# LayerNorm statistics of a dense decoder part: per-token transposes replaced by GpSimd sums and products with 1/1024

## The chip, the cores and the metric

The kernel runs on one core of a Trainium2 chip. The metric is the device time of one execution in microseconds (us), the median of the runs of the same program. The profile is one execution seen by the hardware profiler; its engines are TensorE (PE; PEld is its weight load), VectorE (DVE), ScalarE (ACT), GpSimd (POOL) and SyncE (SP), which issues the DMAs.

## The reference, cut to what matters

Two decoder layers on x of 1024 tokens by 1024 channels, all in float32: layer 0 mixes tokens by a gated DeltaNet, layer 1 by a causal convolution of 31 taps; each is followed by an MLP.

```
def layer_norm(x, g, b):
    mu = mean(x, axis=-1); var = mean(square(x - mu), axis=-1)
    return (x - mu) * rsqrt(var + LN_EPS) * g + b

h = x * (1 + sc1) + sh1
y = deltanet_mixer(h, ...) if layer 0 else conformer_conv_mixer(h, ...)   # the second has a layer_norm of its own
x = layer_norm(ALPHA * x + (1 + gt1) * y, ln_g[i, 0], ln_b[i, 0])
h = x * (1 + sc2) + sh2
x = layer_norm(ALPHA * x + (1 + gt2) * (square(relu(h @ w1)) @ w2), ln_g[i, 1], ln_b[i, 1])
```

There are five LayerNorms in it. The last is done with the output; the four others are done here for each half of the tokens apart, which makes the eight that the change touches.

## The kernel before, in words

Activations lie transposed: a tile is 128 channels by 512 tokens, so eight tiles (k = 0 to 7) hold one half of the tokens (hf = 0 or 1). Each float32 product is done in three passes, with a weight tile split into `whi` and `wlo` and an activation split the same way (lines 234 to 236). A job is one weight tile of 128 by 1024: its load (`raw`), the cast `whi` on ACT, the rest `wlo` on DVE (line 415), 24 products of 512 columns on PE, and what empties the PSUM bank. One job is one unit of planned time (a tick). After the DeltaNet part the program is one list of such jobs: output projections (`dno0`, `dno1`), MLP up and down jobs, convolution inputs (`cfin`), convolution outputs (`cfo0`, `cfo1`). The taps of the convolution are 30 DVE instructions for each tile (line 961).

Every step of a job or a LayerNorm is an event with a planned time; the program sorts the events, and PE, DVE and ACT get their instructions in that order. Nothing waits for a planned time on the chip: each engine takes its instructions in order and waits only for data and buffers. POOL and SP also work in order; the order in which instructions stand there is made by the framework's scheduler.

The eight LayerNorms, in order of time, with the start of their transposes in the trace: `ln00_0` (650 us), `ln00_1` (702), `ln01_0` (1101), `lncf0` (1457), `ln01_1` (1502), `ln10_0` (1549), `lncf1` (1898), `ln10_1` (1993). The digits are layer, place in the layer and half; `cf` is the LayerNorm inside the convolution module. Each goes through these steps in `ln_job`:

- `tok(tt)`, four times: PE turns 128 tokens of the eight tiles round (eight transposes, line 982, four in one PSUM bank), DVE takes `bn_stats` of both banks and `bn_aggr` (lines 986 to 990), POOL makes rsqrt(var + eps) and -mean * rsqrt (lines 991, 256, 993) in columns of `lnst`.
- `rows_`: PE turns `lnst` into rows (line 1018), ACT copies them (1021), and three DMAs bring the rows through DRAM and back, spread over all partitions, as two tiles `lo` of 128 by 512.
- `back(k)`, eight times: DVE multiplies the tile by the first of these (1031) and adds the second (1033); `evac` makes the next activation on ACT (`hh`, the residual `ax`, and once more in `tl`; lines 1067 to 1073) and its rest on DVE (line 246).

While this goes on, PE works on the jobs of the other half. The table `LN` has for each LayerNorm the planned times of these steps, in ticks from its start t0. `resid` (line 259) adds a job's result to the residual tile `ax`. The mod jobs `ada` (line 202, DVE) stand among the first dense jobs.

Of the kernel before, what the change touches and what calls it, by code (L numbers as in the profile page):

```python
# [16 lines left out]
P = 128  # L17
D = 1024
# [71 lines left out]
}  # L90
TOK_AT = (0.0336, 0.0339, 0.0617, 0.4138)
ROWS_AT = (-0.2768, -0.2717)
BACK_AT = (-0.1782, 0.0453, 0.5048, 0.7384, 0.8678, 0.9365)
# [30 lines left out]
def tile_hybrid(ctx, tc, xT, c, adaT, cols, rows, gates, w_gate, w_first, w_dn, w_dno, w_cf, w_cfo,  # L124
# [24 lines left out]
    hb = Bufs("act", tz=3, lo=20)  # L149
    wb = Bufs("weights", raw=3, whi=2, wlo=2)  # L150
    cb = Bufs("const")
    sm = Bufs("small", st=2, mv=2, lnst=2, lnrow=2, rs=2, nb=2, ssk=2, ssq=2, nk=2, br2=6, eq=6, gl=6, ss=3)
    sm("pad", 96)
    dr = ctx.enter_context(tc.tile_pool(name="dr", bufs=1, space=DRAM))

# [723 lines left out]

    def res_post(ps, k, hf, l, j, v):  # L880
# [7 lines left out]
            yield  # L888
        return post

    def out_job(lab, w_dram, k, hf, l, t0, v):
        dense(lab, w_dram[k], t0, 1.0, wide_mm(hf, v), 4, (res_post(0, k, hf, l, 2, v), 1.0, RES_AT))

    def up_job(l, ci, f, hf, hid, t0):
# [32 lines left out]

    def dn_job(l, ci, q, hf, hid, t0):
        ends = (0.75 if q == 0 else 0.5, 1.0)
        dense(f"m{l}_dn{hf}", w_2[l, ci, q], t0, 1.0, hid_mm(hid, q == 0), 4,  # L930
              *[(res_post(j, q * 2 + j, hf, l, 5, ver(hf)), ends[j], RES_AT) for j in range(2)])

    def cf_job(hf, ct, t0):
# [9 lines left out]
        def post():  # L943
# [22 lines left out]
                yield  # L966
        at = max(t0 + 2 + CF_AT[2], conv_end[0])
        conv_end[0] = at + TAP[hf] * (CFK - 1)
        add(f"conv{hf}", post(), t0 + 2 + CF_AT[0], t0 + 2 + CF_AT[1], at,
            *spaced(at + 0.1, conv_end[0] + 0.1, CFK - 1))  # L970

# [91 lines left out]
    def ln_mod(lab, hf, l, which, t0):  # L1063
# [232 lines left out]
```

## Time and profile before

| | us |
|---|---|
| median of 3 runs | 2411.41 (2410.13 to 2414.36) |
| the profiled execution, whole | 2410.48 |
| its span, first to last instruction | 2408.6 |
| PE busy | 2357.5 (98%) |
| DVE busy | 1722.9 (72%) |
| ACT busy | 1100.3 (46%) |
| POOL busy | 409.3 (17%) |

Busy time is the union of an engine's instructions. Products on PE overlap: one of 512 columns shows about 390 ns, and yet 178 of them start in 40 us. So what one costs is read from start to start and not from its length. DVE instructions overlap a little as well (an instruction of 690 ns starts about 600 ns after the one before it). Idle time of an engine means loss only where PE, which has the most to do, stands still for it.

### The profile page before, as it was taken

To read this page: it belongs to the slowest core of one execution; us is meant where nothing else is said; L and a number is where in the kernel's file an instruction comes from. 1 tells how busy PE (TensorE), PEld (TensorE's weight loads), DVE (VectorE), ACT (ScalarE), POOL (GpSimd) and SP (SyncE) were. 2 spreads that over 40 slices of the span, in tenths; PEclk is the share of its full clock that TensorE was granted. 3 is DMA by queue.
4 is the path that set the end of the run, shared out by engine and by line. 5 is a ranking of instruction groups with operands and counts; after the bars stand their busy time and mean duration, and the time that the engine had idled before them with its cause. 6 is when DMAs were issued, how large, how long until landed. Compare 5 with 4: busy or idle time off the path is not lost.

```text
span 2408.6 us, 33443 instructions
## 1 busy us (share of the span) xinstructions
PE 2357.5 (98%) x12730; PEld 1946.2 (81%) x12730; DVE 1722.9 (72%) x2712; ACT 1100.3 (46%) x1949; POOL 409.3 (17%) x841
## 2 busy tenths in 40 slices
PE   8899999999999999999999999999999999999998
PEld 6677878787778888888888888878888888888887
DVE  6667677676686566656899998799888766444447
ACT  4767767564256333335433334563333336333333
POOL 1356556454410000000000001100000001000003
PEclk9999999999999999999999999999999999999999
DMA  8343223334553556542322222222222332222223
GB/s 303 107 131 100 87 66 86 102 102 137 188 159 104 171 186 197 191 155 88 105 97 96 97 96 96 97 97 104 97 96 96 101 118 97 96 97 96 96 97 131
DMA packets 118143, 287.02 MB, mean 119 GB/s; under 512 B 35168, under 2 KB 44768, under 8 KB 117984
## 3 DMA queue, kind: packets, MB, share of 16 engines
q1 hardware_dynamic: 117984, 284.90, 36.3%
q8 instruction: 100, 1.64, 0.3%
q14 instruction: 59, 0.48, 0.1%
HBM read 275.35 MB, written 9.50 MB: 118 GB/s over the span
## 4 chain that ended last, share of the span: by engine, by line
PE 80%; DVE 7%; POOL 5%; DMA 4%; ACT 2%; issue 2%; SPq 0%; DVEq 0%; ACTq 0%; POOLq 0%
PE pd L234 25%; PE pd L236 25%; PE pd L235 24%; POOL T L563 2%; POOL X L565 2%; PE pp L982 1%; DVE wlo L415 1%; DVE tl L1031 1%; DVE lo L246 1%; DVE tl L1033 1%; DMA A<-d_in 1%; DMA d_in<-NT 1%; DMA Xc<-d_out 1%; DVE ax L259 1%; DVE raw L202 1%
## 5 line engine op out<-in xcount | busy, mean ns | idle before, releaser
L234 PE MATMUL pd<-hh,whi 128*128 128x512 f32 x2014 | 817.9, 406 | 6.9 <-DVE ax L259 3.9
L236 PE MATMUL pd<-hh,wlo 128*128 128x512 f32 x2014 | 789.5, 392 | 1.9 <-DVE wlo L415 1.8
L235 PE MATMUL pd<-lo,whi 128*128 128x512 f32 x2014 | 788.4, 391 | 0.6 <-DVE lo L246 0.6
L412 ACT CAST whi<-raw 128x1024 fp32r<-128x1024 f32 x382 | 398.4, 1043 | 544.5 <-PE pd L235 535.1
L415 DVE TENSOR_TENSOR wlo<-raw,whi 128x1024 fp32r<-128x1024 f32 x382 | 468.1, 1226 | 25.9 <-ACT whi L412 23.6
L236 PEld LDWEIGHTS pd<-hh,wlo 128*128 128x128 f32 x2014 | 379.6, 189 | 85.8 <-DVE wlo L415 4.7
L234 PEld LDWEIGHTS pd<-hh,whi 128*128 128x128 f32 x2014 | 381.4, 189 | 78.7 <-issue 3.9
L235 PEld LDWEIGHTS pd<-lo,whi 128*128 128x128 f32 x2014 | 381.6, 189 | 69.7 <-DVE lo L246 1.8
L234 PE MATMUL pd<-xh,whi 128*128 128x512 f32 (+1 forms) x1056 | 404.9, 383 | 0.0
L235 PE MATMUL pd<-xl,whi 128*128 128x512 f32 (+1 forms) x1056 | 404.1, 383 | 0.3 <-DVE xl L246 0.3
L236 PE MATMUL pd<-xh,wlo 128*128 128x512 f32 (+1 forms) x1056 | 404.1, 383 | 0.0
L961 DVE SCALAR_TENSOR_TENSOR cv<-u,col,cv 128x512 f32<-128x512 f32 x480 | 359.1, 749 | 9.6 <-ACT cv L957 1.8
L259 DVE SCALAR_TENSOR_TENSOR ax<-pd,mod,ax 128x512 f32<-128x512 f32 x280 | 208.4, 749 | 154.0 <-PE pd L236 152.9
L246 DVE TENSOR_TENSOR xl<-ts,xh 128x512 fp32r<-128x512 f32 x128 | 88.4, 691 | 256.6 <-ACT ts L905 256.0
L899 ACT ACTIVATE tz<-pd 128x512 f32<-128x512 f32 x128 | 76.6, 599 | 394.9 <-PE pd L236 394.9
L235 PEld LDWEIGHTS pd<-xl,whi 128*128 128x128 f32 x1056 | 198.5, 188 | 39.3 <-DVE xl L246 0.5
L234 PEld LDWEIGHTS pd<-xh,whi 128*128 128x128 f32 x1056 | 198.6, 188 | 38.6
L236 PEld LDWEIGHTS pd<-xh,wlo 128*128 128x128 f32 x1056 | 198.5, 188 | 38.5
L202 DVE CUSTOM_DVE_ANT_0 raw<-raw,condb 128x1024 f32<-128x1024 f32 x96 | 117.9, 1229 | 24.1 <-DMA raw<-in_adaT_dram 23.9
L563 POOL TENSOR_TENSOR T<-X,A 32x15 f32<-32x15 f32 (+7 forms) x240 | 100.1, 417 | 23.9 <-DMA A<-d_in 5.8
L565 POOL TENSOR_TENSOR X<-X,T 32x15 f32<-32x15 f32 (+7 forms) x240 | 99.1, 413 | 18.3
L991 POOL TENSOR_SCALAR lnst<-mv 128x1 f32<-128x1 f32 x32 | 14.9, 465 | 508.6 <-DVE mv L990 338.7
(248 smaller groups left out, 2177.5 us busy)
## 6 DMA issues: line engine op xcount, KB each, us to landing
raw<-in_w_dram SPq DMA_DIRECT2D x260, 512.0 KB, 3.2
raw<-in_adaT_dram SPq DMA_DIRECT2D x96, 512.0 KB, 3.4
raw<-in_w_dn_dram SPq DMA_DIRECT2D x57, 512.0 KB, 3.8
raw<-in_w_cf_dram SPq DMA_DIRECT2D x32, 512.0 KB, 3.2
raw<-in_w_dno_dram SPq DMA_DIRECT2D x16, 512.0 KB, 3.3
raw<-in_w_cfo_dram SPq DMA_DIRECT2D x16, 512.0 KB, 3.2
raw<-in_w_first_dram SPq DMA_DIRECT2D x8, 512.0 KB, 6.5
tz<-in_xT_dram SPq DMA_DIRECT2D x16, 256.0 KB, 5.5
```

The lines of the kernel that those rows point to most:

```text
L202: ve.tensor_tensor_reduce(out=raw, in0=raw, in1=condb, op0=ALU.mult, op1=ALU.add, scale=1.0, scalar=0.0, accum_out=mod[l][j][:, k:k + 1])
L234: te.matmul(ps, lhsT=w[0][:, s_], rhs=ah, start=(first and i == 0), stop=False)
L235: te.matmul(ps, lhsT=w[0][:, s_], rhs=al, start=False, stop=False)
L236: te.matmul(ps, lhsT=w[1][:, s_], rhs=ah, start=False, stop=(last and i == n - 1))
L246: ve.tensor_tensor(lo, x32, hi.bitcast(F32), op=ALU.subtract)
L259: ve.scalar_tensor_tensor(AX[hf][k], ps, g[:, k:k + 1], AX[hf][k], op0=ALU.mult, op1=ALU.add)
L412: sc.copy(hi, raw)
L415: ve.tensor_tensor(lo, raw, hi.bitcast(F32), op=ALU.subtract)
L563: gp.tensor_tensor(t, X[:, 0:i + 1, i:i + 1].broadcast_to(sh), A[:, i:i + 1, i + 1:].broadcast_to(sh), op=ALU.mult)
L565: gp.tensor_tensor(X[:, 0:i + 1, i + 1:], X[:, 0:i + 1, i + 1:], t, op=ALU.subtract)
L899: sc.activation(r, d[0], AF.Relu)
L961: ve.scalar_tensor_tensor(cv, u[:, j:j + HALF], col[:, b_ + j:b_ + j + 1], cv, op0=ALU.mult, op1=ALU.add)
```

## The change

Each tile is added to a running sum as soon as it is complete, the first six additions on POOL, the last on DVE. One product of this sum with a 128 by 128 matrix of 1/1024 (`share`) gives the mean of every token on all partitions. DVE subtracts the mean from the eight tiles in place, ACT squares each, POOL adds the first six squares, DVE the last two, and four small products with a column of `share` give the variance as a column for each 128 tokens. DVE adds eps, POOL takes the power -0.5, PE turns the four columns into rows, and two DMAs instead of three bring one tile `lo` back. `back` then multiplies only. The table `when` holds the planned time at which each tile is complete.

```diff
+    share = cb("share", P)
+    gp.memset(share, 1.0 / D)
-    'ln00_0': (0.077, 0.6353, 3.3, 4.463, 0.3766), 'ln00_1': (0.75, 0.3126, 3.35, 4.1, 0.43),
+    'ln00_0': (0.5, 0.75, 0.22, 2.95, 3.25, 4.3, 0.37), 'ln00_1': (0.5, 0.75, 0.22, 2.95, 3.25, 4.2, 0.4),
...
-        def tok(tt):
-            need(*key, n=n if lab == "ln00_0" else n - 4)
-            if not s:
-                s["st"] = sm("lnst", [2, 4])
-            stats = ln_stats(src[hf], tt, ds[tt], s["st"][:, 0, tt:tt + 1], s["st"][:, 1, tt:tt + 1])
...
+        def sums():
+            for i, k in enumerate(order[1:], 1):
+                need(*key, n=n + i + 1 - KT)
+                r = s["r"] = src[hf]
+                if i == 1:
+                    s["a"] = hb("lo")
+                    gp.tensor_add(s["a"], r[order[0]], r[k])
+                else:
+                    (ve if i == KT - 1 else gp).tensor_tensor(s["a"], s["a"], r[k], op=ALU.add)
+                    did("sum", lab)
+                yield
+        def mean():
+            need("sum", lab, n=KT - 2)
+            s["r"] = list(src[hf])
+            s["m"] = bank("pp")
+            te.matmul(s["m"], lhsT=share, rhs=s["a"], start=True, stop=True)
+            yield
+        def center(i):
+            r = s["r"][order[i]]
+            ve.tensor_tensor(r, r, s["m"], op=ALU.subtract)
+            yield
+            q = s[i] = lb("tl")
+            sc.activation(q, r, AF.Square)
+            yield
+            if i == 1:
+                gp.tensor_add(s["a"], s[0], s[1])
+            elif 1 < i < 6:
+                gp.tensor_add(s["a"], s["a"], q)
+            elif i == 7:
+                ve.tensor_tensor(q, s[6], q, op=ALU.add)
+                ve.tensor_tensor(s["a"], s["a"], q, op=ALU.add)
+            did("square", lab)
+            yield
+        def var():
+            need("square", lab, n=KT)
+            ps = bank("pp")
+            for j in range(4):
+                te.matmul(ps[:, j:j + 1], lhsT=s["a"][:, blk(j)], rhs=share[:, 0:1], start=True, stop=True)
+            yield
+            v = s["v"] = sm("lnst", 4)
+            ve.tensor_scalar(v, ps[:, 0:4], LN_EPS, None, op0=ALU.add)
+            power(v, v, -0.5)
+            yield
         def rows_():
...
-            te.transpose(ps[0:8, 0:P], s["st"].rearrange("p a t -> p (a t)"), ident)
+            te.transpose(ps[0:4, 0:P], s["v"], ident)
...
-            s["b"] = [hb("lo"), hb("lo")]
-            for a in range(2):
-                nc.sync.dma_start(s["b"][a], bass.AP(d.tensor, d.offset + a * HALF, [[0, P], [1, HALF]]))
+            s["b"] = hb("lo")
+            nc.sync.dma_start(s["b"], bass.AP(d.tensor, d.offset, [[0, P], [1, HALF]]))
...
-            ve.tensor_tensor(t, s["r"][k], s["b"][0], op=ALU.mult)
-            yield
-            ve.tensor_tensor(t, t, s["b"][1], op=ALU.add)
+            ve.tensor_tensor(t, s["r"][k], s["b"], op=ALU.mult)
```

Line numbers in the changed kernel are higher: 1024 and 1021 are the sums, 1032 the mean, 1057 the variance, 1060 the eps, 1066 the rows, 235 to 237 the three passes, 247, 257 and 260 what 246, 256 and 259 were.

On PE, at the end of the statistics of `ln00_0`, in the program before the rows (`lnst`) follow the last product of a `dno1` job, with the 32 transposes long past:

```order
L235 MATMUL pd_7889<-lo_7568,whi_7780 128x512
L236 MATMUL pd_7889<-hh_1_1537_7567,wlo_7788 128x512
L234 MATMUL pd_7889<-hh_1_1541_7601,whi_7780 128x512
L235 MATMUL pd_7889<-lo_7602,whi_7780 128x512
L236 MATMUL pd_7889<-hh_1_1541_7601,wlo_7788 128x512
L1018 MATMUL pp_7931<-ident_471,lnst_7744 8x128
L234 MATMUL pd_7941<-hh_1_1488_7348,whi_7852 128x512
```

In the changed program the products for the variance (`share`) stand where a `dno1` job ends (its bank is `pd_7860`), and the rows six products behind them:

```order
L236 MATMUL pd_7860<-lo_7602,whi_7773 128x512
L237 MATMUL pd_7860<-hh_1_1541_7601,wlo_7781 128x512
L1057 MATMUL pp_7902<-share_7621,lo_7634 128x1 x4
L235 MATMUL pd_7912<-hh_1_1488_7348,whi_7829 128x512
L236 MATMUL pd_7912<-lo_7349,whi_7829 128x512
L237 MATMUL pd_7912<-hh_1_1488_7348,wlo_7839 128x512
L235 MATMUL pd_7912<-hh_1_1494_7376,whi_7829 128x512
L236 MATMUL pd_7912<-lo_7377,whi_7829 128x512
L237 MATMUL pd_7912<-hh_1_1494_7376,wlo_7839 128x512
L1066 MATMUL pp_7921<-ident_471,lnst_7909 4x128
```

So the power on POOL has six products of 512 columns between the variance and the rows; before, no such pair stood on PE.

On POOL at the same place, before, there are three small instructions for each 128 tokens and nothing else:

```order
L991 TENSOR_SCALAR lnst_7744<-mv_7819 128x1
L256 TENSOR_TENSOR lnst_7744<-lnst_7744,expo_103_482 128x1
L993 TENSOR_SCALAR lnst_7744<-mv_7819,lnst_7744 128x1
L991 TENSOR_SCALAR lnst_7744<-mv_7863 128x1
L256 TENSOR_TENSOR lnst_7744<-lnst_7744,expo_103_482 128x1
L993 TENSOR_SCALAR lnst_7744<-mv_7863,lnst_7744 128x1
```

Now the squares of `ln00_0` (sum `lo_7634`) are followed by the first sums of `ln00_1` (`lo_7856`), and the power of `ln00_0` (`lnst_7909`) stands behind the second of them, which takes the tile `ax_1_1557` of the `dno1` job above (its bank is `pd_7860`):

```order
L1046 TENSOR_TENSOR lo_7634<-lo_7634,tl_7841 128x512
L1046 TENSOR_TENSOR lo_7634<-lo_7634,tl_7853 128x512
L1021 TENSOR_TENSOR lo_7856<-ax_1_1552_7642,ax_1_1553_7645 128x512
L1024 TENSOR_TENSOR lo_7856<-lo_7856,ax_1_1557_7654 128x512
L257 TENSOR_TENSOR lnst_7909<-lnst_7909,expo_103_482 128x4
L1024 TENSOR_TENSOR lo_7856<-lo_7856,ax_1_1559_7659 128x512
```

The same order stands once more, where `ln01_1` ends and the sums of `ln10_0` begin. On DVE in the changed program the tile `ax_1_1557` and the eps come in this order:

```order
L1049 TENSOR_TENSOR lo_7634<-lo_7634,tl_7878 128x512
L416 TENSOR_TENSOR wlo_7892<-raw_7792,whi_7884 128x1024
L260 SCALAR_TENSOR_TENSOR ax_1_1557_7654<-pd_7860,mod_2_5_75,ax_1_1557_7654 128x512
L1060 TENSOR_SCALAR lnst_7909<-pp_7902 128x4
L203 ISA raw_7867,mod_5_8_78<-raw_7867,condb_85 128x1024
```

The last addition of the squares (1049) is two places ahead of the residual of that job, and an `ada` instruction is right behind the eps.

## Rows read from the trace of the kernel before

**Rows 1.** The page: busy time of PE, and the chain that ended last by engine.
```profile
PE 2357.5 (98%) x12730; PEld 1946.2 (81%) x12730; DVE 1722.9 (72%) x2712; ACT 1100.3 (46%) x1949; POOL 409.3 (17%) x841
PE 80%; DVE 7%; POOL 5%; DMA 4%; ACT 2%; issue 2%; SPq 0%; DVEq 0%; ACTq 0%; POOLq 0%
```

**Rows 2.** Waits of PE, 640 to 2340 us: us in total, times, longest.
```profile
PE pp L982 <- DVE ax L259: 2.5, 2, 2.2
...
PE pp L1018 <- POOL lnst L993: 0.5, 1, 0.5
```

**Rows 3.** Stretches: us, then busy time and count by engine, granted clock, DMA share, GB/s.
```profile
1400.00:1440.00 40.00, 40.00 (x178) 33.10 (x178) 37.41 (x50) 14.94 (x21) 0.57 (x1) 1.00 0.28 93
1440.00:1480.00 40.00, 40.00 (x195) 33.34 (x194) 29.41 (x42) 14.62 (x21) 7.43 (x13) 1.00 0.29 96
...
708.00:711.00 3.00, 3.00 (x12) 2.62 (x11) 2.90 (x6) 2.23 (x4) 0.00 (x0) 0.57 0.78 238
```

**Rows 4.** PE in order of time at `lncf0`: start us, length us, instruction.
```profile
1457.41 1.03 PE L982 MATMUL pp<-ident,cv 128*128 128x128 f32 x8
1458.20 0.48 PE L234 MATMUL pd<-hh,whi 128*128 128x512 f32 x1
1458.52 0.40 PE L235 MATMUL pd<-lo,whi 128*128 128x512 f32 x1
```

**Rows 5.** PE in order of time: four float32 products, eight instructions.
```profile
79.58 1.05 PE L501 MATMUL pp<-k 128*128 128x128 f32 x8
80.39 0.47 PE L234 MATMUL pd<-hh,whi 128*128 128x512 f32 x1
80.71 0.40 PE L235 MATMUL pd<-lo,whi 128*128 128x512 f32 x1
```

**Rows 6.** PE in order of time, the wait at `ln00_1` (idle before, releaser).
```profile
705.67 0.33 PE L982 MATMUL pp<-ident,ax 128*128 128x128 f32 x1 [2.24 <-DVE ax L259]
```

**Rows 7.** Groups by line, 640 to 2340 us: busy us, mean ns, idle before.
```profile
L259 DVE SCALAR_TENSOR_TENSOR ax<-pd,mod,ax 128x512 f32<-128x512 f32 x272 | 202.4, 749 | 150.9 <-PE pd L236 149.7
...
L1033 DVE TENSOR_TENSOR tl<-tl,lo 128x512 f32<-128x512 f32 x64 | 44.1, 689 | 0.6
...
L986 DVE BATCH_NORM_STATS2 st<-pp 128x6 f32<-128x512 f32 x32 | 22.2, 695 | 23.1 <-PE pp L982 23.0
...
L902 ACT ACTIVATE xh<-tz 128x512 fp32r<-128x512 f32 x124 | 78.4, 632 | 3.9
```

**Rows 8.** DVE in order of time, two instructions of 512 columns back to back.
```profile
1497.67 0.69 DVE L1033 TENSOR_TENSOR tl<-tl,lo 128x512 f32<-128x512 f32 x1
1498.27 0.69 DVE L1031 TENSOR_TENSOR tl<-cv,lo 128x512 f32<-128x512 f32 x1
```

**Rows 9.** POOL, single lines: length ns min/median/max, first and last start us, forms.
```profile
L1183 POOL TENSOR_TENSOR lo<-lo,cv x4: 1260/1445/1857, 2349.1 to 2401.9; 128x512 f32<-128x512 f32 x4
L256 POOL TENSOR_TENSOR ss<-ss,expo x16: 1006/1007/1978, 175.7 to 630.4; 128x4 f32<-128x4 f32 x16
```

**Rows 10.** POOL in order of time near the end of the span.
```profile
2401.90 1.26 POOL L1183 TENSOR_TENSOR lo<-lo,cv 128x512 f32<-128x512 f32 x1
2403.24 1.59 POOL L1184 TENSOR_TENSOR lo<-lo,cv 128x512 f32<-128x512 f32 x1
```

**Rows 11.** DVE at the same place.
```profile
2400.41 0.75 DVE L1187 SCALAR_TENSOR_TENSOR lo<-lo,rs,cv 128x512 f32<-128x512 f32 x1
...
2401.92 1.78 DVE L1187 SCALAR_TENSOR_TENSOR lo<-lo,rs,cv 128x512 f32<-128x512 f32 x1
2403.63 0.74 DVE L1186 SCALAR_TENSOR_TENSOR lo<-pp,mv,cv 128x512 f32<-128x512 f32 x1
```

**Rows 12.** All engines in order of time at `ln01_0`: the rows on their way.
```profile
1117.90 0.27 PE L1018 MATMUL pp<-ident,lnst 128*8 128x128 f32 x1
...
1118.21 0.25 ACT L1021 COPY lnrow<-pp 8x128 f32<-8x128 f32 x1 [2.83 <-PE pp L1018]
...
1123.18 0.69 DVE L1031 TENSOR_TENSOR tl<-ax,lo 128x512 f32<-128x512 f32 x1 [0.84 <-DMA lo<-lnd]
```

More of the change, by code (lines that the diff above doesn't have):

```diff
@@ L85 @@
 LN = {
[4 rows of a table removed]
-}
-TOK_AT = (0.0336, 0.0339, 0.0617, 0.4138)
-ROWS_AT = (-0.2768, -0.2717)
-BACK_AT = (-0.1782, 0.0453, 0.5048, 0.7384, 0.8678, 0.9365)
[4 rows of a table added]
+}
+SQ_AT = (0.0, 0.12, 0.22)
+VAR_AT = (0.0, 0.09)
+ROWS_AT = (0.0, 0.02)
+BACK_AT = (-0.02, 0.3, 0.53, 0.7, 0.85)
 LAST_AT = (
@@ L151, in tile_hybrid @@
     cb = Bufs("const")
-    sm = Bufs("small", st=2, mv=2, lnst=2, lnrow=2, rs=2, nb=2, ssk=2, ssq=2, nk=2, br2=6, eq=6, gl=6, ss=3)
+    sm = Bufs("small", st=2, mv=2, lnst=2, lnrow=1, rs=2, nb=2, ssk=2, ssq=2, nk=2, br2=6, eq=6, gl=6, ss=3)
     sm("pad", 96)
@@ L889, in res_post @@
         return post
+    when = {(n, hf): [-2.5] * KT for n in ("ax", "cv") for hf in range(2)}
     def out_job(lab, w_dram, k, hf, l, t0, v):
+        when["ax", hf][k] = t0 + 1.0 + RES_AT[0]
         dense(lab, w_dram[k], t0, 1.0, wide_mm(hf, v), 4, (res_post(0, k, hf, l, 2, v), 1.0, RES_AT))
@@ L929, in dn_job @@
         ends = (0.75 if q == 0 else 0.5, 1.0)
+        for j in range(2):
+            when["ax", hf][q * 2 + j] = t0 + ends[j] + RES_AT[0]
         dense(f"m{l}_dn{hf}", w_2[l, ci, q], t0, 1.0, hid_mm(hid, q == 0), 4,
@@ L968, in cf_job @@
         conv_end[0] = at + TAP[hf] * (CFK - 1)
+        when["cv", hf][ct] = conv_end[0] + 0.1
         add(f"conv{hf}", post(), t0 + 2 + CF_AT[0], t0 + 2 + CF_AT[1], at,
@@ L997, in ln_job @@
     def ln_job(lab, hf, src, evac, t0):
-        n_ax = goal.get(("ax", hf), 0)
         key = ("cv" if src is CV else "ax", hf)
-        n = KT if src is CV else n_ax
-        s, ds = {}, [{} for _ in range(4)]
-        def tok(tt):
-            need(*key, n=n if lab == "ln00_0" else n - 4)
-            if not s:
-                s["st"] = sm("lnst", [2, 4])
-            stats = ln_stats(src[hf], tt, ds[tt], s["st"][:, 0, tt:tt + 1], s["st"][:, 1, tt:tt + 1])
-            for i, _ in enumerate(stats):
-                yield
-                if i == 1:
-                    need(*key, n=n)
+        n = KT if src is CV else goal.get(("ax", hf), 0)
@@ new lines, in ln_job @@
+        at = list(when[key])
+        order = sorted(range(KT), key=lambda k: at[k])
+        s = {}
+        def sums():
[8 more added lines that the diff above has]
+                    did("sum", lab)
+                yield
@@ L1014, in rows_ @@
+        def var():
[8 more added lines that the diff above has]
+            yield
         def rows_():
-            assert all("rs" in d for d in ds)
-            s["r"] = list(src[hf])
@@ L1017, in rows_ @@
             ps = bank("pp")
-            te.transpose(ps[0:8, 0:P], s["st"].rearrange("p a t -> p (a t)"), ident)
+            te.transpose(ps[0:4, 0:P], s["v"], ident)
             yield
-            t = sm("lnrow", P, p=8)
-            sc.copy(t, ps[0:8, 0:P])
-            d = dr.tile([8, P], F32, name=nm("lnd"), tag="lnd", bufs=2)
+            t = sm("lnrow", P, p=4)
+            sc.copy(t, ps[0:4, 0:P])
+            d = dr.tile([4, P], F32, name=nm("lnd"), tag="lnd", bufs=2)
             nc.sync.dma_start(d, t)
-            s["b"] = [hb("lo"), hb("lo")]
@@ L1030, in back @@
             t = lb("tl")
-            ve.tensor_tensor(t, s["r"][k], s["b"][0], op=ALU.mult)
-            yield
-            ve.tensor_tensor(t, t, s["b"][1], op=ALU.add)
+            ve.tensor_tensor(t, s["r"][k], s["b"], op=ALU.mult)
             yield
             yield from evac(k, t)
-        at, tok_p, rows_t, back_t, back_p = LN[lab]
-        for tt in range(4):
-            add(lab, tok(tt), *[t0 + at + tt * tok_p + o for o in TOK_AT])
+        mean_t, diff_t, diff_p, var_t, rows_t, back_t, back_p = LN[lab]
+        add(lab, sums(), *[at[k] + 0.001 for k in order[1:]])
+        add(lab, mean(), t0 + mean_t)
+        for i in range(KT):
+            add(lab, center(i), *[t0 + diff_t + i * diff_p + o for o in SQ_AT])
+        add(lab, var(), *[t0 + var_t + o for o in VAR_AT])
         add(lab, rows_(), *[t0 + rows_t + o for o in ROWS_AT])
@@ L1080, in ln_mod @@
             seen.add((l, which))
-            add(lab, once(mod_cols, l, which), t0 + LN[lab][3] - 3.0)
+            add(lab, once(mod_cols, l, which), t0 + LN[lab][5] - 3.0)
         ln_job(lab, hf, AX, evac, t0)
```

6 rows, old and new, of the table LN are left out of this document.

## The prediction

> **What bounds the kernel now.** I read the page first: PE is busy for 98% of the span, and the chain that ended last runs on PE for 80% [rows 1]. Then the waits of PE over the stretch in which the eight LayerNorms lie: they are so few that the longest entry is 2.5 us in 1700 [rows 2]. Then the stretches of 40 us: where no LayerNorm is, 178 products of 512 columns start in 40 us with no gap, 0.225 us each, at granted clock 1.00 [rows 3]. So the dense part is bound by PE's own work. Two things count: how much PE has to do, and whether PE, which works in order, has to stand for what other engines bring. DVE, ACT and POOL matter only through the second.
>
> One place stands out. At `ln00_1` a transpose waits 2.24 us for a residual from a DVE that is behind [rows 6]; after it the granted clock is 0.57 over 708 to 711 us, between its levels of 1.2 and 2.4 GHz [rows 3], so that 3.0 us do the work of 1.7 and 1.3 us go.
>
> **PE work that goes.** Each LayerNorm has 32 transposes in groups of eight. From the start of a group to the next product are 0.79 us, and that product takes 0.32 to the next start and not 0.225, as the engine goes over to other weights [rows 4]: 0.88 us for a group, 4 x 0.88 = 3.5 for a LayerNorm. The stretches agree: 1440 to 1480 us has 195 instructions with 33 short ones, so 162 x 0.225 = 36.4 us of products, and 3.6 for the short ones [rows 3]. Eight LayerNorms: 28.2 us. The turn of the rows stays.
>
> **PE work that comes.** A float32 product that isn't a transpose is two instructions here: the eight rows of 128 columns at 79.58 us take 0.81 us, and 0.09 more on the product behind them [rows 5]. The mean has two instructions of 512 columns, as many columns as those eight: 0.90 us. The variance has eight instructions of one column each, but each has a whole 128 x 128 tile of weights to load: if the load sets the pace, 0.90 us again. The trace does not show which of both sets it. From below: two products at the pace of the three-pass ones, 0.45 us, and a variance that is free. I take 1.8 us for each LayerNorm, the nearest rows, 14.4 in all (bounds 3.6 and 14.4). PE's work falls by 13.8 us (at most by 24.6).
>
> **Other engines.** DVE loses 64 `bn_stats` of 0.695 and 64 additions of 0.689 us, 88.6 us [rows 7], and the small aggregations; it gains 88 instructions of 0.69. That is 28 us less and lies beside PE. ACT gains 64 squares at 0.63 us, 40 us, beside PE as well. POOL gains 88 additions at 1.26 us or more [rows 9], 111 us, in a stretch where it did next to nothing. None of this is on the path by itself; it lengthens or shortens the chains below.
>
> **Waits that go.** The 2.5 and 0.5 us for transposes and rows [rows 2], and the slow clock behind the first, 1.3: 4.3 us (bounds 0, when the mean waits for the same DVE, and 4.3).
>
> **Waits that come.** There are three new places where PE stands behind a chain.
>
> First the rows: variance, eps on DVE, power on POOL, turn on PE, with six products, 1.35 us, between. DVE is a small instruction (0.2), the power of 128 x 4 takes 1.01 us [rows 9], the end of the products and three handoffs take about 0.4 (in [rows 12] the copy starts 0.04 us after the turn has ended, 0.31 after it began): 1.6 us, so 0.3 us of wait. DVE has a `wlo` or `xl` around the eps, and the power was as long as 1.98 us at times [rows 9]; I take 0.5 us for six LayerNorms: 3.0.
>
> Second, in `ln00_0` and `ln01_1` the power is queued on POOL behind a sum that takes the residual of the job which ends right ahead of the variance. From that job's end: its result 0.2, residual 0.75 [rows 7], sum 1.26 and power 1.01 [rows 9], handoffs 0.3: 3.5 us, against 0.9 + 1.35 on PE. That is 1.3 us; with the power at 1.98 it is 2.2. I take 1.8 twice, 3.6, and one slow clock of 1.3. Behind the power stand POOL's next sums and, through PE, everything.
>
> Third the mean and the variance. The mean stands 12 products, 2.7 us, behind a LayerNorm's last job; residual and last sum take 0.2 + 0.75 + 0.69, so it is on time unless DVE is behind. In `ln00_1` it will be: the last `lo` of `ln00_0` stands ahead of that residual on DVE. I take 1.5 us there and 0.5 for all the others. The variance I followed through for `ln01_0`, from the end of its last job: mean ready at 3.8, three subtractions until 5.7 at 0.6 each [rows 8]; DVE then holds the `xl` of an up job that ends at 6.3, and its relu and two squares, three ACT instructions of about 0.63 [rows 7], end at 8.4; five more subtractions and a `wlo` until 13.3; the relu and squares of the next up job stand ahead of the last square on ACT, so that this one ends at 13.5 + 3 x 0.63 + 0.63 = 16.0, and DVE's two additions at 17.3. POOL has its last square at 12.8 and is done by 14.3. PE comes to the variance after 72 products and the mean, at 17.1: 0.4 us late. Three LayerNorms stand like this, 1.2 us; in the others the squares have ACT for themselves.
>
> Together 3.0 + 4.9 + 2.0 + 1.2 = 11.1 us (bounds 2, when every chain is hidden, and over 30, below). The row vector then needs 5 us from the copy to DVE (1118.21 to 1123.18 us) [rows 12], as before; the passes behind it have one DVE instruction less in each tile.
>
> **The sum.** -13.8 - 4.3 + 11.1 = -7.0 us on the profiled execution of 2410.48 (span 2408.6 and 1.9 around it): 2403.5. The median of the runs is 0.9 above that execution: 2404.4, 0.29% faster.
>
> **Rivals.**
>
> Even: the waits that come take what PE's work gives back. It needs 7 us more of them, 0.9 us for each LayerNorm, as when DVE or ACT comes to each chain with one long instruction in hand (`wlo`, 1.2 us). For it speaks that every chain has a slack under 1 us; against it that PE's waits on DVE and ACT are so rare now [rows 2]. 2411.
>
> Slower, by the POOL additions and DVE in each other's way. An instruction on DVE with two inputs in SBUF took 0.75 us alone and 1.78 us when POOL's addition, 2401.90 to 2403.16, ran beside it [rows 10, 11]: it ended 0.5 us after POOL, so it had stood until POOL was done. POOL's own addition went from 1.26 to 1.86 us in other cases [rows 9]. If each of the five additions of squares holds DVE for 1.03 us and grows by 0.6, the last sum of squares comes up to 5 us later, less about 2 us of slack on DVE: 3 us of wait at each variance, 24 us, and a slow clock of 1.3 behind each, 10: 2404.4 + 34 = 2438. It decides from 0.9 us for each LayerNorm on (7 us). Against it: the subtractions, most of DVE's work there, take one input from PSUM, and a DVE instruction of that kind, at 2403.63, kept its 0.74 us beside POOL's of 2403.24 to 2404.83. The Trainium skill (SBUF — State Buffer, Who interferes with whom) says that an instruction with two SBUF inputs and a GpSimd instruction that reads SBUF shut each other out for their whole length, and one with a single SBUF input does not contend. By that rule the 1.78 us is what is to be expected, the trace agrees, and `wlo`, `xl` and the taps would suffer, the subtractions not.
>
> Much faster: the chains are hidden after all, or the products are cheap. With 2 us of new waits -13.8 - 4.3 + 2 = -16.1, 2395; with products at the lower bound, 10.8 less, 2384.
>
> **Chances.** My forecast 0.47 (its own range 2398 to 2407), much faster 0.10, even 0.30, slower 0.13. Within 0.2%, 2406.6 to 2416.2, is about what a measurement of this kernel cannot tell from no change. A tenth of the even case I count on either side of it, and 0.02 of my forecast within: faster 0.45 + 0.10 + 0.03 = 0.58, same 0.02 + 0.24 = 0.26, slower 0.03 + 0.13 = 0.16. The range that should hold eight in ten, 2393 to 2415, takes in the even case and the hidden chains, and leaves out the slow case and the cheapest products.
>
> **What would show it.** Right: two instructions at the mean that together take about 0.9 us to the next product, the variance the same; stretches with a LayerNorm that hold 7 or 8 products of 512 columns more than before in their time; PE's longest new waits at the rows of `ln00_0` and `ln01_1`, for POOL's power, 1.3 to 2.2 us; waits under 1 us at the other rows. Wrong: waits of 2 us or more at the variance in most LayerNorms, with POOL's additions at 1.8 us and DVE's `wlo` at over 2; or a mean and variance that cost PE 3 us and more.

## The result and the profile after

The changed kernel takes 2430.61 us (median of 4 runs, 2429.59 to 2432.02) against 2412.18 for the kernel before (4 runs beside it): 0.8% slower, ratio 1.0079, 95% interval 1.0067 to 1.0091. The forecast was 2404.4, and its range ended at 2415.

The profiled execution took 2430.61 us itself. The page, as in [rows 1]: busy time of the engines, then the chain that ended last.

```profile
PE 2352.6 (97%) x12554; PEld 1934.5 (80%) x12554; DVE 1724.0 (71%) x2648; ACT 1133.9 (47%) x2013; POOL 518.2 (21%) x842
...
PE 76%; DVE 8%; POOL 6%; ACT 4%; DMA 3%; issue 2%; SPq 0%; DVEq 0%; ACTq 0%; POOLq 0%
```

Two numbers are to be seen. PE's share of the chain fell from 80 to 76%, so PE stands still more. And DVE is as busy as before, 1724.0 against 1722.9 us, though it has some 28 us less to do.

The waits of PE over the stretch of [rows 2], in us in total, times, longest:

```profile
PE pp L1032 <- DVE lo L1024: 11.0, 3, 5.3
PE pp L1057 <- DVE lo L1049: 9.2, 7, 2.5
PE pp L1066 <- POOL lnst L257: 7.1, 5, 2.6
```

L1032 is the mean, L1057 the variance, L1066 the rows. They wait 27.3 us in all, and from 645 us on all waits of PE come to 27.7; in the kernel before they came to 4.9 there.

The stretches that answer to [rows 3]: one of 40 us without a LayerNorm, one with `lncf0`, and 2.4 us in `ln01_0` behind a wait (columns as there).

```profile
1409.00:1449.00 40.00, 40.00 (x178) 33.15 (x177) 38.53 (x50) 15.29 (x21) 2.29 (x2) 1.00 0.28 92
1449.00:1489.00 40.00, 38.62 (x172) 30.86 (x171) 30.85 (x42) 18.09 (x28) 9.31 (x7) 1.00 0.30 98
...
1126.00:1128.40 2.40, 2.40 (x6) 1.68 (x7) 0.70 (x2) 0.00 (x0) 1.40 (x1) 0.50 0.65 217
```

Without a LayerNorm nothing has changed: 178 products. With one, the 32 transposes are gone and ten instructions have come (two for the mean, eight for the variance; the turn of the rows stays), yet there are 161 products of 512 columns of the jobs where there were 162: 1.4 us of idle time took what the shorter work gave. And after PE stood for 1.22 us at the variance of `ln01_0` the granted clock is 0.50, 1.2 GHz, and six products take 2.4 us instead of 1.35.

PE in order of time, as in [rows 4, 5]: the mean of `lncf1`, then the variance of `ln10_0`, both without a long wait.

```profile
1915.66 1.02 PE L1032 MATMUL pp<-lo,share 128*128 128x512 f32 x2
1916.12 0.80 PE L235 MATMUL pd<-xh,whi 128*128 128x512 f32 x1
1916.76 0.40 PE L236 MATMUL pd<-xl,whi 128*128 128x512 f32 x1
...
1580.92 1.05 PE L1057 MATMUL pp<-share,lo 128*128 128x1 f32 x8
1581.84 0.48 PE L235 MATMUL pd<-hh,whi 128*128 128x512 f32 x1
1582.15 0.40 PE L236 MATMUL pd<-lo,whi 128*128 128x512 f32 x1
```

From the start of the mean to the second product behind it are 1.10 us, of which one product's 0.227 is its own: the mean costs 0.87. For the variance that is 1.23 - 0.23 = 1.00. So PE's own work came out as forecast.

The rows of `ln00_0`, on POOL and PE: the power stands in POOL's queue behind a sum, as forecast.

```profile
673.75 2.17 POOL L1024 TENSOR_TENSOR lo<-lo,ax 128x512 f32<-128x512 f32 x1 [3.35 <-DVE lnst L1060]
675.88 1.03 POOL L257 TENSOR_TENSOR lnst<-lnst,expo 128x4 f32<-128x4 f32 x1
```
```profile
676.97 0.27 PE L1066 MATMUL pp<-ident,lnst 128*4 128x128 f32 x1 [2.58 <-POOL lnst L257]
```

Now the longest wait, at the mean of `ln01_1`. DVE, POOL and PE in order of time (start us, length us, instruction, idle before):

```profile
1499.29 1.78 DVE L247 TENSOR_TENSOR lo<-tl,hh 128x512 fp32r<-128x512 f32 x1
...
1510.52 2.28 DVE L416 TENSOR_TENSOR wlo<-raw,whi 128x1024 fp32r<-128x1024 f32 x1
...
1513.33 0.74 DVE L260 SCALAR_TENSOR_TENSOR ax<-pd,mod,ax 128x512 f32<-128x512 f32 x1
1514.18 0.69 DVE L1024 TENSOR_TENSOR lo<-lo,ax 128x512 f32<-128x512 f32 x1
```
```profile
1498.91 1.61 POOL L1024 TENSOR_TENSOR lo<-lo,ax 128x512 f32<-128x512 f32 x1 [3.10 <-DVE ax L260]
```
```profile
1515.02 2.04 PE L1032 MATMUL pp<-lo,share 128*128 128x512 f32 x2 [5.34 <-DVE lo L1024]
```

DVE has work without a gap here: the passes of `lncf0` (L1078, L247), weights (L416) and the residuals (L260) that POOL adds up. The `lo` of 1499.29 takes 1.78 us and not 0.68: it ends 0.55 us after POOL's addition (1500.52), as in [rows 10, 11]. Between 1495 and 1515 us five DVE instructions are longer in this way, by 0.50, 1.10, 1.10, 1.11 and 1.06: 4.9 us, and the last residual comes that much late. PE waits 5.3. Over the whole stretch DVE's instructions are 29.8 us longer in sum than the lower quartile of their kind (counting those that exceed it by over 0.15 us), and POOL's 29.3. In the kernel before POOL's were 20.6 us longer already, but DVE has no such instruction there.

The other kind of lateness shows at the variance of `ln01_0`, on ACT and DVE:

```profile
1120.77 0.58 ACT L906 ACTIVATE tz<-pd 128x512 f32<-128x512 f32 x1
...
1122.43 0.62 ACT L1040 ACTIVATE tl<-ax 128x512 f32<-128x512 f32 x1
```
```profile
1117.39 1.55 DVE L416 TENSOR_TENSOR wlo<-raw,whi 128x1024 fp32r<-128x1024 f32 x1 [1.04 <-ACT whi L413]
...
1122.56 0.69 DVE L247 TENSOR_TENSOR xl<-ts,xh 128x512 fp32r<-128x512 f32 x1 [1.83 <-ACT ts L912]
1123.17 0.68 DVE L1048 TENSOR_TENSOR tl<-tl,tl 128x512 f32<-128x512 f32 x1
1123.96 0.69 DVE L1049 TENSOR_TENSOR lo<-lo,tl 128x512 f32<-128x512 f32 x1
```

The last square (L1040) stands on ACT behind the relu and the two squares of an up job, DVE's two additions behind that job's `xl`, and PE's variance starts at 1124.70. POOL's last addition of squares had ended at 1121.64, so it is not POOL's sum that is waited for. Ahead of all this DVE had stood 1.04 us for a `whi`, and its `wlo` was 0.33 us longer beside a POOL addition; the subtractions behind it, and with them the squares, came that much later.

### The profile page after: what moved, and what is told of

It reads as the page before. It is cut to its first block, busy times and chain, and to the rows that moved or that the text cites. A ratio compares the mean times of both kernels' runs of the same rounds, so it can differ in the third digit from the quotient of the medians.

```text
span 2428.8 us, 33158 instructions
## 1 busy us (share of the span) xinstructions
PE 2352.6 (97%) x12554; PEld 1934.5 (80%) x12554; DVE 1724.0 (71%) x2648; ACT 1133.9 (47%) x2013; POOL 518.2 (21%) x842
## 4 chain that ended last, share of the span: by engine, by line
PE 76%; DVE 8%; POOL 6%; ACT 4%; DMA 3%; issue 2%; SPq 0%; DVEq 0%; ACTq 0%; POOLq 0%
PE pd L235 23%; PE pd L237 23%; PE pd L236 23%; POOL T L564 2%; POOL X L566 2%; DVE wlo L416 2%; DVE lo L247 1%; ACT whi L413 1%; DMA Xc<-d_out 1%; DVE tl L1078 1%; DVE ax L1037 1%; DVE cv L970 0%; ACT tl L1040 0%; DVE ax L260 0%; DVE raw L203 0%
## 5 line engine op out<-in xcount | busy, mean ns | idle before, releaser
L416 DVE TENSOR_TENSOR wlo<-raw,whi 128x1024 fp32r<-128x1024 f32 x382 | 474.7, 1243 | 57.9 <-ACT whi L413 55.4
L970 DVE SCALAR_TENSOR_TENSOR cv<-u,col,cv 128x512 f32<-128x512 f32 x480 | 364.7, 761 | 9.9 <-ACT cv L966 2.1
L260 DVE SCALAR_TENSOR_TENSOR ax<-pd,mod,ax 128x512 f32<-128x512 f32 x280 | 207.7, 747 | 151.8 <-PE pd L237 150.9
L247 DVE TENSOR_TENSOR xl<-ts,xh 128x512 fp32r<-128x512 f32 x128 | 89.5, 699 | 248.0 <-ACT ts L912 247.9
L564 POOL TENSOR_TENSOR T<-X,A 32x15 f32<-32x15 f32 (+7 forms) x240 | 103.0, 429 | 22.8 <-DMA A<-d_in 4.7
L1024 POOL TENSOR_TENSOR lo<-lo,cv 128x512 f32<-128x512 f32 x10 | 17.4, 1735 | 323.6 <-DVE cv L970 323.6
```

Source lines behind the costliest of these rows:

```text
L247: ve.tensor_tensor(lo, x32, hi.bitcast(F32), op=ALU.subtract)
L260: ve.scalar_tensor_tensor(AX[hf][k], ps, g[:, k:k + 1], AX[hf][k], op0=ALU.mult, op1=ALU.add)
L416: ve.tensor_tensor(lo, raw, hi.bitcast(F32), op=ALU.subtract)
L564: gp.tensor_tensor(t, X[:, 0:i + 1, i:i + 1].broadcast_to(sh), A[:, i:i + 1, i + 1:].broadcast_to(sh), op=ALU.mult)
L970: ve.scalar_tensor_tensor(cv, u[:, j:j + HALF], col[:, b_ + j:b_ + j + 1], cv, op0=ALU.mult, op1=ALU.add)
```

## The experiments

Two theories. *Collisions*: POOL's additions and DVE instructions that read two tiles from SBUF hold each other up, DVE gets late, and PE waits. *Places*: the table of times puts mean, variance and rows too early for chains of that length, whatever POOL does. All ratios are to the kernel before on the same chip; waits are PE's idle time over 645 to 2340 us (after 27.7, before 4.9). The expectations count the same waits from start to start: 31 us in all, mean 11.8, variance 10.4, rows 8.9.

### no_pool, no_sums: POOL's additions left out

The first part of the diff is no_sums; no_pool has both.

```diff
-                    gp.tensor_add(s["a"], r[order[0]], r[k])
...
-                    (ve if i == KT - 1 else gp).tensor_tensor(s["a"], s["a"], r[k], op=ALU.add)
+                    if i == KT - 1:
+                        ve.tensor_tensor(s["a"], r[order[0]], r[k], op=ALU.add)
...
-            if i == 1:
-                gp.tensor_add(s["a"], s[0], s[1])
-            elif 1 < i < 6:
-                gp.tensor_add(s["a"], s["a"], q)
-            elif i == 7:
+            if i == 7:
                 ve.tensor_tensor(q, s[6], q, op=ALU.add)
-                ve.tensor_tensor(s["a"], s["a"], q, op=ALU.add)
+                ve.tensor_tensor(s["a"], s[5], q, op=ALU.add)
```

> POOL's 88 additions of 128 x 512 are left out (the mean is taken from two tiles and the variance from three; DVE's three additions of each LayerNorm, all products, subtractions, squares and all places stay). Collision theory: in the changed kernel's trace DVE's instructions of the dense part are 29.8 us longer in sum than the quickest of their kind, all of it beside POOL's additions, where in the kernel before they are 0.0 us longer; DVE is late at the residuals and at the squares for that reason, and PE's 31 us of waits at mean, variance and rows follow. With the additions gone DVE's 29.8 us go, PE's waits fall under 10 us with the slow clock behind them, and the time is 2404 to 2412. Places theory: the chains from subtraction to square to sum are planned too early whatever POOL does; PE's waits stay over 20 us, and the time is 2422 to 2430.

> Only POOL's 48 additions of tiles for the mean are left out (the mean is taken from two tiles; the additions of squares on POOL stay). Collision theory: the longest waits, 11.8 us at the mean, come from DVE instructions held up beside these additions (in ln01_1 three of about 1.1 us and two wlo of 0.5 and 1.05 between 1495 and 1513 us, 5.0 us against a wait of 5.3); they fall to 4 us or less, and the rows lose the 3.5 us that stand behind a sum on POOL; with the slow clock behind both the time falls by 11 to 16 us, to 2415 to 2420. Places theory: DVE is late because its places beside the passes of the LayerNorm ahead are too tight; the mean's waits stay within 3 us of 11.8 and the time falls by 5 us at most.

no_pool: 2408.81 us, ratio 0.9988 (0.9979 to 0.9996), DVE busy 1695.6, waits 13.8. no_sums: 2417.71, 1.0018 (1.0008 to 1.0029), waits 17.6. DVE in no_pool at the place shown above, and PE's waits there:

```profile
1497.83 0.69 DVE L247 TENSOR_TENSOR lo<-tl,hh 128x512 fp32r<-128x512 f32 x1
1498.43 0.75 DVE L260 SCALAR_TENSOR_TENSOR ax<-pd,mod,ax 128x512 f32<-128x512 f32 x1
1499.21 0.69 DVE L1023 TENSOR_TENSOR lo<-ax,ax 128x512 f32<-128x512 f32 x1
```
```profile
PE pp L1061 <- POOL lnst L257: 5.2, 7, 1.7
PE pp L1031 <- DVE lo L1023: 4.4, 2, 3.0
PE pp L1052 <- DVE lo L1044: 4.2, 4, 1.8
```

The additions cost 21.8 us, 12.9 of it those for the mean (the interval of no_sums leaves some 3 us of doubt in this split), and the long wait at the mean of `ln01_1` is gone in no_pool and 0.4 us in no_sums. Both totals are in the ranges of the collision theory. But no_pool's waits were to fall under 10 and are 13.8, and those at no_sums' means to 4 or less and are 4.8: the means of `ln00_1` and `ln10_0` (3.0 and 1.4) wait without any POOL addition, as do some variances and rows. Collisions are not all.

### dummy_pool: the additions stay, nobody waits for them

```diff
-                    (ve if i == KT - 1 else gp).tensor_tensor(s["a"], s["a"], r[k], op=ALU.add)
+                    if i == KT - 1:
+                        s["c"] = lb("tl")
+                        ve.tensor_tensor(s["c"], r[order[0]], r[k], op=ALU.add)
+                    else:
+                        gp.tensor_tensor(s["a"], s["a"], r[k], op=ALU.add)
...
-            te.matmul(s["m"], lhsT=share, rhs=s["a"], start=True, stop=True)
+            te.matmul(s["m"], lhsT=share, rhs=s["c"], start=True, stop=True)
...
-                ve.tensor_tensor(s["a"], s["a"], q, op=ALU.add)
+                ve.tensor_tensor(q, s[5], q, op=ALU.add)
...
-                te.matmul(ps[:, j:j + 1], lhsT=s["a"][:, blk(j)], rhs=share[:, 0:1], start=True, stop=True)
+                te.matmul(ps[:, j:j + 1], lhsT=s[7][:, blk(j)], rhs=share[:, 0:1], start=True, stop=True)
```

> All POOL additions stay in number and place, but nobody waits for what they add up: DVE's last addition before the mean takes the first and the last tile into a buffer of its own, and the last two before the variance add three squares (what is computed is that of no_pool). So their collisions with DVE stay and the waits for POOL's results go. If the 21.8 us that came off without POOL's additions (2430.6 to 2408.8) are collisions, DVE's instructions are again about 30 us longer in sum and the time is 2425 to 2431. If they are waits for POOL's sums, it is 2408 to 2414.

2429.5 us, ratio 1.0071 (1.0059 to 1.0084); DVE's instructions are 32.0 us longer, and the waits are those of the changed kernel:

```profile
PE pp L1036 <- DVE tl L1026: 10.5, 3, 5.0
PE pp L1061 <- DVE tl L1053: 9.2, 7, 2.5
PE pp L1070 <- POOL lnst L257: 7.7, 7, 2.5
```

So the additions don't cost by the waits for their results: between the medians that is 1.1 us, less than the two intervals, each about 6 us wide, can tell from nothing. Two things are left, and this run keeps both: DVE's instructions are held up beside the additions, and the power stands behind additions in POOL's queue. power_first, below, takes the second away at `ln00_0` and `ln01_1` and is 4.5 us faster; the greater part of the 21.8 is the first.

### sum_dve: the additions for the mean on DVE

```diff
-                    gp.tensor_add(s["a"], r[order[0]], r[k])
+                    ve.tensor_add(s["a"], r[order[0]], r[k])
...
-                    (ve if i == KT - 1 else gp).tensor_tensor(s["a"], s["a"], r[k], op=ALU.add)
+                    ve.tensor_tensor(s["a"], s["a"], r[k], op=ALU.add)
```

> The 48 additions of tiles for the mean move from POOL to DVE, with the same places; the squares stay on POOL. DVE takes 48 x 0.60 = 29 us more work. Collision theory: an addition of POOL costs a DVE with work in hand about 1.0 us, more than doing it there (0.60), so DVE is no later than now at the crowded residuals, the mean's waits fall from 11.8 to 6 or less, and power on POOL has no sum ahead of it (rows 8.9 to 5): time 2416 to 2423. Places theory: DVE is the late engine, and 29 us more on it make the mean's waits longer than 11.8: 2432 or more.

2432.44 us, ratio 1.0086 (1.0074 to 1.0099): a miss for the collision theory as I had priced it, and just inside the range of the places theory, though the waits at the mean grew from 11.0 to 11.3 us only. (The profiled execution was the slowest of five, 2438.32 us.) DVE's collisions fell to 6.0 us, but its own 29 us took their place (busy 1731.3), and the mean waits as long:

```profile
PE pp L1032 <- DVE lo L1024: 11.3, 3, 4.8
```

At `ln01_1` the wait fell from 5.3 to about 4.0, at `ln10_0` it rose from 1.5 to 2.5, and five additions put ahead of `wlo` at the start of the dense part (642 us) made PE wait 3.8 us more there. Behind that the same products fall back by 18.0 us, just as in the changed kernel. What counts at these means is how late DVE is; whether additions or collisions make it late is the same to PE.

### power_first, fast_center, table2: places alone

power_first:

```diff
-VAR_AT = (0.0, 0.09)
+VAR_AT = (0.0, 0.045)
```

fast_center, the same number in all eight:

```diff
-    'ln01_0': (0.5, 0.75, 0.22, 2.95, 3.25, 4.3, 0.37), 'ln01_1': (0.5, 0.75, 0.22, 2.95, 3.25, 4.3, 0.37),
+    'ln01_0': (0.5, 0.75, 0.16, 2.95, 3.25, 4.3, 0.37), 'ln01_1': (0.5, 0.75, 0.16, 2.95, 3.25, 4.3, 0.37),
```

table2, which has power_first's line too; the first six numbers of `ln01_1` stand in `ln00_1` and `ln10_0` as well, and those of `ln01_0` in the rest:

```diff
+    'ln01_0': (0.5, 0.7, 0.16, 2.85, 3.3, 4.35, 0.37),
+    'ln01_1': (1.2, 1.4, 0.15, 3.2, 3.65, 4.7, 0.37),
```

> eps and power of every LayerNorm take their places 0.045 of a job (0.24 us) sooner, which puts the power of ln00_0 and of ln01_1 ahead of the sum on POOL and eps ahead of the residual on DVE; nothing else moves in these two. If the queue on POOL sets the rows' wait there, 2.74 and 1.81 us fall to 1.0 and 0.5 (eps 0.2, power 1.0, turn, against 1.35 us of products), the slow clock behind the first goes in part, and the time falls by 3 to 5 us, to 2426 to 2428. If the row's wait is the chain's own length, it stays within 0.5 us and the time with it.

> Only the step between two subtractions goes from 0.22 to 0.16 of a job, which puts the last square ahead of the second up job's relu and squares on ACT (in ln01_0 the last square ended at 1123.05 behind them, 1.6 us before the variance could start, while POOL had been done at 1121.6). Places theory: the waits at the variance, 10.4 us, fall to 4 or less: 2420 to 2426. If POOL's additions set them, they stay within 2 us, and so does the time.

> Only places in the table of times change: the mean of ln00_1, ln01_1 and ln10_0 0.7 of a job later (3.8 us; their waits at the mean are 4.3, 5.5 and 1.7), the subtractions 0.15 or 0.16 of a job apart instead of 0.22, so that the last square stands ahead of the next up job's relu on ACT; variance 0.1 sooner or, in the three, 0.25 later; rows 0.45 behind the variance instead of 0.30, eps and power ahead of the sum on POOL; passes behind the row vector up to 0.5 later. Places theory: PE's waits fall from 31 to under 12 us with most of the slow clock behind them: 2403 to 2412. Collision theory: as many additions on POOL beside a DVE that is as full, so the waits move to the new places: 2420 or more.

power_first: 2426.1 us, ratio 1.0052 (1.004 to 1.0064). The rows of `ln00_0` and `ln01_1` no longer wait long (0.2 and 0.0 us instead of 2.7 and 1.8, from start to start). This wait was the queue: POOL's sum ahead of the power, and to a smaller part the residual (0.66 us) ahead of the eps on DVE, which the edit moves as well.

fast_center: 2418.48, ratio 1.0023 (1.0012 to 1.0033), with all additions and 34 us of collisions in place. On ACT, at `ln01_0`, the last square now stands ahead of the relu:

```profile
1118.24 0.63 ACT L1040 ACTIVATE tl<-ax 128x512 f32<-128x512 f32 x1 [1.22 <-DVE ax L1037]
1118.78 0.58 ACT L906 ACTIVATE tz<-pd 128x512 f32<-128x512 f32 x1
```
```profile
PE pp L1032 <- DVE lo L1024: 10.7, 3, 5.3
PE pp L1066 <- POOL lnst L257: 8.5, 4, 4.0
PE pp L1057 <- DVE lo L1049: 2.0, 2, 1.3
```

The variance's 9.2 us are 2.0. One number, the same in all eight LayerNorms, was worth 12.1 us, more than the places theory gave it (2420 to 2426); PE's waits as a whole fell by 6.3, and the time at granted clock 0.50 by 6.8 us. The rows of `ln00_0` got worse (4.0 us).

table2: 2419.31, ratio 1.0026 (1.0018 to 1.0035), neither theory's range. The waits at the mean are gone, but 16.3 of the 27.7 us are left: 10.3 at the variance, where 9.2 were, and 4.8 at products of the next jobs (L240) for `lo` passes that now come late. Moving the mean gained nothing over fast_center:

```profile
PE pp L1061 <- DVE lo L1053: 10.3, 6, 2.7
PE pd L240 <- DVE lo L251: 4.8, 5, 2.9
```

### table2_no_pool: both

Its edits are those of table2 and of no_pool.

> table2 without POOL's 88 additions (left out as in no_pool). What is left of the change is its work on PE, and the waits that places and collisions together don't explain. PE's work alone, 13.3 us less, and the 4.3 us of waits that are gone give 2412.9 - 17.6 = 2395; with 2 to 8 us of waits left 2397 to 2403. 2406 or more would mean that a third cause holds PE up.

2393.55 us, ratio 0.9924 (0.9911 to 0.9938), waits 4.4. Places alone took 11.3, the additions alone 21.8, and both together 37.1, a little more than their sum. It is below the range I gave (2397 to 2403). In the profiled executions the same products come 15.1 us earlier at the end than in the kernel before: PE's work explains 13.2 and the waits, 4.4 against 4.9, another 0.5; 1.4 us are not accounted for (between the medians it is 19.3, with runs from 2390.43 to 2400.3). So nothing else holds PE up. It leaves the additions out, so it is a bound and no version.

### table3, mixed: versions that compute everything

table3, the table and who adds (mixed has the same table; both have power_first's line too):

```diff
+    'ln00_0': (0.5, 0.7, 0.16, 2.955, 3.4, 4.45, 0.37),
+    'ln00_1': (1.2, 1.4, 0.13, 3.3, 3.75, 4.75, 0.37),
+    'ln01_0': (0.5, 0.75, 0.16, 2.95, 3.25, 4.3, 0.37),
+    'ln01_1': (1.1, 1.25, 0.14, 2.955, 3.45, 4.4, 0.37),
+    'lncf0': (0.5, 0.75, 0.16, 2.95, 3.25, 4.3, 0.37),
+    'lncf1': (0.5, 0.7, 0.16, 2.95, 3.35, 4.3, 0.44),
+    'ln10_0': (0.85, 1.05, 0.16, 3.0, 3.55, 4.5, 0.37),
+    'ln10_1': (0.5, 0.75, 0.16, 2.95, 3.25, 4.1, 0.45),
...
-                    gp.tensor_add(s["a"], r[order[0]], r[k])
+                    (ve if lab == "ln01_1" else gp).tensor_add(s["a"], r[order[0]], r[k])
...
-                    (ve if i == KT - 1 else gp).tensor_tensor(s["a"], s["a"], r[k], op=ALU.add)
+                    (ve if i == KT - 1 or lab == "ln01_1" else gp).tensor_tensor(s["a"], s["a"], r[k], op=ALU.add)
```

mixed, where `ln_job_tok` is `ln_job` of the kernel before, with its table entries for these two:

```diff
+LN_TOK = {'ln01_1': (0.7274, 0.4273, 3.0443, 4.3616, 0.3873), 'ln10_0': (0.3567, 0.5683, 3.1074, 4.1425, 0.3701)}
...
+        if lab in LN_TOK:
+            return ln_job_tok(lab, hf, src, evac, t0)
```

> The whole of the change, with places taken for each LayerNorm from what fast_center and table2 showed (subtractions 0.13 to 0.16 of a job apart, mean of ln00_1, ln01_1 and ln10_0 0.35 to 0.7 later, rows 0.30 to 0.55 behind the variance), and the additions for the mean of ln01_1 on DVE, which is full there (four collisions of about 1.1 us against four additions of 0.60). If places and collisions are what costs, the dense part loses less than in fast_center (2418.5) and table2 (2419.3): 2406 to 2413. If waits only move from one place to the next, 2415 or more.

> The change in six LayerNorms with the places of table3; ln01_1 and ln10_0, where DVE is full of the passes of the LayerNorm ahead, keep the transpositions and bn_stats of the kernel before, so no addition of POOL lies beside those passes. PE's work falls by six LayerNorms' share of 13.3 us, 10 us, and the waits of the kernel before at ln00_1 go. By the sum of the LayerNorms' own lags in fast_center and table2 (00_0 +0.5, 00_1 -2.7, 01_0 -2.5, cf0 -1.5, cf1 -1.2, 10_1 -1.8, the two others 0) the time is 9 us under the kernel before: 2401 to 2407. If collisions cost elsewhere what they cost in the two, 2411 or more.

table3: 2413.07 us, ratio 1.0009 (1.0000 to 1.0017): 17.5 us better than the changed kernel, at the upper end of its range (2406 to 2413), and no better than the kernel before; 15.6 us of waits are left. mixed: 2405.58, ratio 0.9972 (0.9961 to 0.9982), faster than both kernels. Its waits are 6.6 us in all, the longest at the variance:

```profile
PE pp L1115 <- DVE lo L1107: 4.4, 3, 2.8
```

What the two given back cost shows in how far the same products fall behind the kernel before over `ln01_1` and `ln10_0` (products that start there between 1485 and 1600 us): 7.4 us in the changed kernel, and with other places still 8.2 (fast_center), 8.1 (table2) and 8.0 (table3); without POOL's sums for the mean they come 1.1 earlier (no_sums), and in mixed 1.3. So in these two, where DVE is full of the passes of the LayerNorm ahead, no table that was tried makes the change pay, and neither do the additions for the mean of `ln01_1` on DVE (table3). In the other six mixed gains 6.1 us.

## Why the prediction was wrong

The dense part itself lost 18.0 us: the same product starts 2.2 us later than in the kernel before at 649 us, ahead of the first mean, and 20.2 later at the end (the 2.2 is no more than executions differ there: 0.0 to 2.7 us in ten of the eleven kernels). The forecast for this part was -7.0, so 25.0 us were missed. The step that failed is the third of the waits that come, mean and variance: 3.2 us were taken for them and 20.2 came, 17.0 of the miss; the slow clock behind such waits is another 8.4, and all other terms together came 0.4 better. Of the signs that were named, the cost of mean and variance on PE came; the longest new waits lie at the means and not at the rows of `ln00_0` and `ln01_1`, and the stretch with `lncf0` holds one product less and not 7 or 8 more.

- **PE's work, -13.8**: right. 8 x (0.87 + 1.00) = 15.0 came against 28.2 that went: -13.2. Where the variance did not wait (fast_center) it took 0.90, the value taken. Why the product behind a group of short ones takes 0.09 us longer, no row shows; the sum needs only the time.
- **Rows, 3.0 + 3.6**: 7.1, right in sum, and by luck in part. At `ln00_0` the wait is 2.6 us where 1.8 were taken, with POOL's sum at 2.17 us and not 1.26 ahead of the power; power_first shows that queue to be the cause. Where 0.5 each were taken, `ln10_0` has 1.7 and `lncf0` 1.0, and three do not wait.
- **Mean, 2.0**: this step failed, with 11.0. "It is on time unless DVE is behind" was the right condition, and I looked at DVE only in `ln00_1`. There 4.2 us came where 1.5 were taken (and where the kernel before had 2.24); `ln01_1` has 5.3 and `ln10_0` 1.5. I gave these 0.5 for all others together. I had followed DVE's queue without the collisions beside the passes of the LayerNorm ahead, where POOL's sums fall. That is 6.6 of the 11.0; the other 4.4 stay without any POOL addition (no_pool: `ln00_1` 3.0, `ln10_0` 1.4) and are DVE's own queue, sized too small.
- **Variance, 1.2**: failed, with 9.2 in seven LayerNorms, not three. I walked the chain for one and found 0.4 us; there 1.2 were measured. That walk took five subtractions and a `wlo` as one run on DVE; in the trace DVE stands 1.04 us for the `whi` of that `wlo`, which is 0.33 longer beside a POOL addition, so ACT comes to the relu ahead of the last square about 1 us later than forecast. "In the others the squares have ACT for themselves" overlooked DVE: in `ln00_0`, where 2.2 us came, its instructions ahead of the last two additions are 2.8 us longer beside POOL's additions, and without these (no_pool) it does not wait. Of the 9.2, no_pool leaves 4.2 and fast_center 2.0, so the collisions and the places each have a part.
- **Waits that go, 4.3**: they went with the transposes, but the mean of `ln00_1` now waits longer for the same DVE; the bound 0 had named that case.
- **Slow clock, 1.3**: 18.0 + 13.2 - 22.8 of net waits leaves 8.4 us by subtraction, products at the 0.50 of the row above and starts after a wait. The traces agree: behind 645 us the granted clock stands at 0.50 for 17.1 us longer in all than in the kernel before, and half of that is 8.5. It was priced behind one wait; it followed others of 1.2 us and more as well (granted clock 0.57 over 1934 to 1938 us, 0.50 over 2030 to 2033), though not the 1.2 us at 729 us.

Of the rivals, *slower* was the right mechanism with its place wrong, and half of the story: of PE's 27.7 us of waits 13.8 stay without the additions. I put the collisions at the sums of squares, 24 us, and let the sums for the mean go free of them; measured, the sums for the mean cost 12.9 (with up to 4.5 for the queue ahead of the power, which was priced) and the squares 8.9. What I held against it was true and not enough: the subtractions, which read the mean from PSUM, were never held up. The 64 of them, by line, shortest, median and longest in ns:

```profile
L1037 DVE TENSOR_TENSOR ax<-ax,pp x48: 670/678/689, 656.5 to 2024.4; 128x512 f32<-128x512 f32 x48
L1037 DVE TENSOR_TENSOR cv<-cv,pp x16: 673/677/689, 1467.4 to 1928.3; 128x512 f32<-128x512 f32 x16
```

The rule that the forecast quoted from the Trainium skill (SBUF — State Buffer, Who interferes with whom) agrees with these and with the 1.78 us of `lo` alike; I named `wlo`, `xl` and the taps as those who suffer, and put no price on any. Of DVE's 29.8 us these three have 7.5, 1.1 and 6.3; left out were `lo` with 7.0, the one-column `mod` with 4.8 and `tl` with 2.9.

## What to carry to other kernels

A step taken off the bounding engine and put on two idle ones pays only if the chain of those that it now waits for is short at each place, so walk every place and not one, and look at what the engine in the middle has in hand there. An addition on POOL cost DVE up to 1.1 us where DVE was full of instructions with two inputs in SBUF, nothing beside those that read PSUM, and on average over the 48 sums 0.5 (29.8 less 6.0 us), hardly less than the 0.60 of doing it on DVE. Where an order is written out as a table of times, try the places before the mechanism is judged: here they were worth 11 to 12 us of the 18, and in two places of eight no table that was tried made the mechanism pay.

## What the runs showed of the hardware

- POOL holds up small DVE instructions as much as long ones: one of a single column took 1.13 us beside POOL's additions and 0.16 elsewhere. It ended at 663.03 us, and the POOL addition that had started before it at 663.02; so it is not the work that counts but the wait for POOL's instruction to end.

```profile
660.94 2.08 POOL L1046 TENSOR_TENSOR lo<-lo,tl 128x512 f32<-128x512 f32 x1 [1.16 <-ACT tl L1040]
661.91 1.13 DVE L207 SCALAR_TENSOR_TENSOR mod<-mod,col 128x1 f32<-128x1 f32 x1
662.96 0.67 DVE L1037 TENSOR_TENSOR ax<-ax,pp 128x512 f32<-128x512 f32 x1
663.55 1.92 DVE L416 TENSOR_TENSOR wlo<-raw,whi 128x1024 fp32r<-128x1024 f32 x1
```

- The other way round too: POOL's power of four columns took 1.94 us at 1934.09, beside a `wlo` that ran from 1933.92 to 1935.15, and 1.02 alone.
- Eight float32 instructions of one column each took PE as long as two of 512 columns, 0.90 to 1.00 us against 0.87. So it is not their columns that set the pace.
